# A two-layer decoder trunk: the first pair of seven-product steps of a feed-forward stage one step later, and a combination's scaling three units behind it

## The chip, the cores and the metric

One core of a Trainium2 chip runs the whole program in one launch. The metric is device microseconds of that core, as the median of several runs. Engine names are those of the profile: PE multiplies matrices (PEld is its weight load), DVE and ACT are the two elementwise engines, POOL here mostly issues transfers, SP issues the weight loads. Instructions of one engine run in the order in which the program emits them; engines wait for each other through semaphores.

## What is computed

The reference, cut to what matters here, for 256 tokens, model width 2048 and two layers:

```
for l in range(DEPTH):
    h = rms_norm(x, norm1_g[l])
    z = h @ w_in[l]
    ...
    x = x + mix @ w_out[l]
    h2 = rms_norm(x, norm2_g[l])
    x = x + jnp.square(jax.nn.relu(h2 @ w_up[l])) @ w_down[l]
return rms_norm(x, final_g)
```

`w_up` is 2048 x 8192 and `w_down` 8192 x 2048. The change touches the last line of the loop alone, the feed-forward part.

## The kernel before

**Weights and their split.** Each float32 weight tile is split into a high part (ACT, `hi`, L167 or L185) and the rest (DVE, `lo`, L177 or L190), and each product is three matmuls: high by high, low by high, high by low. The unit of planning is one weight tile of 128 x 1024 numbers. SP loads it into one of 7 `raw` buffers; there are 6 `hi` and 6 `lo` buffers. The main loop (L993 to L1014) emits, ahead of the matmuls of a step, the `hi` of tiles up to five ahead and the `lo` of tiles up to four ahead.

**Plain steps.** `transposed` (L369) makes channel-major steps: one weight tile as the stationary operand, 24 matmuls (L400, L402, L404), results with channels on the partitions. Here they are called plain steps.

**Seven-product steps.** `fast` (L407) does a 512-column part of `w_down` for one stage with Strassen-like sums: seven products in place of eight, with tokens on the partitions. Each such part is a pair of steps, p = 0 and p = 1. A step has four tiles: top, bottom, and two sums of weights (upper, lower) that DVE makes from the raw tiles in place (L218, L219 ahead of the upper `hi`, L222, L223 behind it). It issues 36 matmuls (L430, L432, L433); the six of its seventh product are held back (`left_over`) and come in the plain step behind it, after that step's first three.

**The stages.** The hidden width is cut into 8 stages of 1024. Stage e computes its part of `w_up` (16 plain steps, four per 256 columns) and uses the hidden values of stage e - 1 for `w_down`: some plain steps, and three pairs (groups 0, 1 and 2, for output columns 0 to 511, 512 to 1023 and 1024 to 1535). Before which plain steps of a stage the two steps of each pair stand is a table (L63 to L66): `USUAL` for stages 2 to 6, `ORDER` for stages 1, 7 and 8. In a usual stage group 1 stands before plain steps 1 and 2, group 2 before 6 and 7, group 0 before 11 and 14. In stage 7 group 1 stands before 1 and 2, group 0 before 6 and 9, and there is no group 2. Plain steps 0 to 3 make up the first 256 columns of `w_up`; behind step 3 their result is taken out of PSUM (L780, or L782 in stage 7), squared (L783) and split (L640 on ACT, L643 on DVE).

**Sums of the activations.** The products of a pair also need sums of hidden values; `sums` (L793) makes them on DVE (L796 to L799), and `parts` splits them (L640 and L643 on the tile `shared`). They are emitted near the end of a stage and are first used by group 1 of the next.

**Results of the pairs.** Groups 1 and 2 accumulate over stages in DRAM (`far`): behind the second step of a pair `other_done` (L879) copies three PSUM banks to `stage` (L897, three ACT instructions), two steps later the seventh product (L883), and POOL adds them to `far` (L862), or in the last stage of a group adds `far` to `stage` (L893). Group 0 stays in PSUM.

**The combination.** When a group is complete (group 2 in stage 6, groups 1 and 0 in stage 7), `combine` (L808) adds the seven products on DVE (L814 to L822), scales the four results by the squared norm factor on ACT (L825), and some units later `turn_back` transposes them on PE (L835) and adds them to `x` (L499). `soon(n, fn)` emits `fn` at the first step that starts at least n units later; a plain step is one unit, a seven-product step four.

Of the kernel before, what the change touches and what calls it, by code (L numbers as in the profile page):

```python
# [31 lines left out]
AF = mybir.ActivationFunctionType  # L32
# [27 lines left out]

ORDER = {1: ((7, 10), (13, 14)), 7: ((6, 9), (1, 2)), 8: ()}  # L63
FINAL = (7, 7, 6)
LAST = (4, 6, 8, 10, 0, 2, 12, 14)
USUAL = ((11, 14), (1, 2), (6, 7))  # L66
WARM = 11
HALVES = 5
D_SCORES, D_NORM, D_TURN, D_VALUES = 2, 1, 3, 2
# [21 lines left out]
def trunk(ctx: ExitStack, tc: tile.TileContext, layout, xT, consts, gains, w, b_sp, w_sp, out):  # L91
# [11 lines left out]
    vec, act, pe = nc.vector, nc.scalar, nc.tensor  # L103
# [142 lines left out]
    def soon(delay, fn):  # L246

        due.append((now[0] + delay, fn))
# [258 lines left out]
    def layer(l, n1, n2, n3, last):  # L507
# [218 lines left out]
        d = 0  # L726
        if l == 0:
            d = 9
# [79 lines left out]
        def combine(place, c, banks, o=None):  # L808

            d1, d2, d3, d5, d7, d6, d4 = (place[:, 256 * n:256 * (n + 1)] for n in range(7))  # L810
            p1, p2, p3, p5, p7, p6, p4 = o or (d1, d2, d3, d5, d7, d6, d4)
            if o:
                act.activation(d1, p1, AF.Copy)
            vec.tensor_tensor(d2, d1, p2, op=OP.add)  # L814
            vec.tensor_tensor(d6, d1, p6, op=OP.add)
            vec.tensor_tensor(d7, d6, p7, op=OP.add)
            vec.tensor_tensor(d6, d6, p5, op=OP.add)
            vec.tensor_tensor(d3, d6, p3, op=OP.add)
            vec.tensor_tensor(d4, d7, d4, op=OP.subtract)
            if o:  # L820
                vec.tensor_tensor(d4, d4, p4, op=OP.subtract)
            vec.tensor_tensor(d7, d7, p5, op=OP.add)  # L822
            for tt, out in enumerate(((d2, d3), (d4, d7))):
                for d in out:
                    act.activation(d, d, AF.Copy, scale=n2.r2[:, tt:tt + 1])  # L825
            wait = 6 if o else 7
            soon(wait, lambda: turn_back(c, d2, d4, banks[0]))
            soon(wait + (1 if o else 2), lambda: turn_back(c + 2, d3, d7, banks[1]))

        def turn_back(c, first, second, bank):  # L830
            ps = bank()
            for j in range(2):
                for tt, src in enumerate((first, second)):
                    o = j * S + tt * P
                    pe.transpose(ps[:, o:o + P], src[:, j * P:(j + 1) * P], ident)  # L835
            soon(1, lambda: update(n3, c, ps, False, last))
# [31 lines left out]
        def first_done(e):  # L868
            def f(o):
                if e < 7:  # L870
                    soon(5, lambda: seventh_out(e, o))
                else:
                    soon(10, lambda: nc.gpsimd.dma_start(stage[:, 1536:1792], far[0]))
                    soon(14, lambda: combine(stage, 0, [aux_bank] * 2, o))
                    for i, c in enumerate((12, 14)):
                        soon(17 + 2 * i, lambda c=c: rest_in(c))
            return f

        def other_done(e, g, banks):  # L879
            here = [lambda i=i: acc_bank(i) for i in (2, 3)]  # L880

            def rest(o):
                act.activation(stage[:, 1536:1792], o[6], AF.Copy)  # L883
                for i in range(4):
                    soon(2 * i, lambda r=slice(512 * i, min(512 * (i + 1), 1792)): move(r))
                if e == FINAL[g]:
                    soon(9, lambda: combine(stage, 4 * g, here))

            def move(r):
                if e < FINAL[g]:  # L890
                    put(e, g, r)
                else:
                    nc.gpsimd.dma_start(stage[:, r], far[g][:, r], accum_op=OP.add)  # L893

            def f(o):
                for i in (2, 0, 1):
                    act.activation(stage[:, 512 * i:512 * (i + 1)], banks[i], AF.Copy)  # L897
                soon(5, lambda: rest(o))
            return f

        base = len(steps)
        for e in range(9):
# [3 lines left out]
            if e:  # L906
                w = 512 * len(ORDER.get(e, USUAL))
                hidden = [hid[e - 1]]
# [3 lines left out]
                               cols=None if e < 8 else [c * P for c in LAST])  # L912
                for g, at in enumerate(ORDER.get(e, USUAL)):
                    banks = []
# [147 lines left out]
```

## Time and profile before

| | us |
|---|---|
| three runs | 2038.5, 2039.89, 2045.22 (median 2039.89) |
| the profiled execution: its own time | 2044.94 |
| its span (first to last instruction) | 2042.6 |
| PE busy in the span | 2027.5 (99%) |
| DVE busy | 1579.3 (77%) |
| ACT busy | 1214.8 (59%) |
| POOL busy | 156.8 (8%) |

The span is 2.3 us shorter than the execution's own time; the profiled execution was 5.05 us above the median of the runs. A row of the timeline gives the start in the span, the duration, engine, line, operation, output and inputs, shapes, and the idle time ahead of it with what ended it. Equal instructions without a gap are merged (x2): the duration is then from the first one's start to the last one's end, and neighbours overlap a little.

### The profile page before, as it was taken

What the parts mean: (1) busy time and instruction counts of PE and PEld (TensorE: products, weight loads), DVE (VectorE), ACT (ScalarE), POOL (GpSimd) and SP (SyncE); (2) the same over time, 40 slices, a digit from 0 to 9 for tenths busy, and PEclk for the clock granted to TensorE, in tenths of its full rate; (3) what the DMA queues carried; (4) which work ended last, traced back from release to release, by engine and by line L of the source; (5) the groups of instructions that cost most, each with busy time, mean ns of one, the idle gap of its engine ahead of it and who ended that gap; (6) DMA issues with size and microseconds to landing.
All of it is one profiled execution on the core that took longest, in us unless ns stands there. A gap on an engine that the chain in (4) does not pass through costs nothing.

```text
span 2042.6 us, 40747 instructions
## 1 busy us (share of the span) xinstructions
PE 2027.5 (99%) x16834; PEld 1988.6 (97%) x16834; DVE 1579.3 (77%) x1950; ACT 1214.8 (59%) x1613; POOL 156.8 (8%) x200
## 2 busy tenths in 40 slices
PE   9999999999999999999999999999999999999997
PEld 8998999999999999999989989999999999999997
DVE  7566765788888888888855667667888888888985
ACT  7565455666675665765545554556665766667654
POOL 0002300001010010100000023000010100100000
PEclk9999999999999999999999999999999999999999
DMA  9555556567586776865565555555676866868562
GB/s 326 191 166 167 184 193 203 168 233 220 196 260 206 227 220 193 241 214 202 197 216 172 169 176 191 191 191 178 217 231 199 272 190 216 256 197 259 184 217 84
DMA packets 126442, 419.26 MB, mean 205 GB/s; under 512 B 14128, under 2 KB 22064, under 8 KB 126256
## 3 DMA queue, kind: packets, MB, share of 16 engines
q1 hardware_dynamic: 110800, 389.86, 56.3%
q0 software_dynamic: 14304, 23.86, 6.4%
q8 instruction: 131, 2.15, 0.4%
q10 hardware_dynamic: 1152, 2.94, 0.4%
q14 instruction: 55, 0.45, 0.1%
HBM read 394.58 MB, written 22.02 MB: 204 GB/s over the span
## 4 chain that ended last, share of the span: by engine, by line
PE 91%; DVE 5%; ACT 2%; issue 1%; DMA 1%; ACTq 0%; DVEq 0%; SPq 0%
PE acc L402 22%; PE acc L404 22%; PE acc L400 22%; PE acc L461 3%; PE acc L459 3%; PE acc L460 3%; PE aux L430 3%; PE aux L433 3%; PE aux L432 3%; PE acc L430 2%; PE acc L432 2%; PE acc L433 2%; DVE lo L177 2%; ACT hi L167 1%; DVE shared L643 1%
## 5 line engine op out<-in xcount | busy, mean ns | idle before, releaser
L167 ACT ACTIVATE hi<-raw 128x1024 fp32r<-128x1024 f32 (+1 forms) x817 | 836.8, 1050 | 516.2 <-DVE raw L219 233.9
L177 DVE TENSOR_TENSOR lo<-raw,hi 128x1024 fp32r<-128x1024 f32 (+1 forms) x817 | 965.0, 1213 | 155.8 <-ACT hi L167 153.6
L400 PE MATMUL acc<-hs,hi 128*128 128x256 f32 x2816 | 784.4, 279 | 0.0
L402 PE MATMUL acc<-hs,lo 128*128 128x256 f32 x2816 | 782.5, 278 | 0.4
L404 PE MATMUL acc<-hs,hi 128*128 128x256 f32 x2816 | 781.3, 277 | 0.0
L402 PEld LDWEIGHTS acc<-hs,lo 128*128 128x128 f32 x2816 | 529.2, 188 | 2.7 <-DVE lo L177 2.0
L400 PEld LDWEIGHTS acc<-hs,hi 128*128 128x128 f32 x2816 | 530.8, 189 | 0.4 <-issue 0.2
L404 PEld LDWEIGHTS acc<-hs,hi 128*128 128x128 f32 x2816 | 529.0, 188 | 0.0
L400 PE MATMUL acc<-half,hi 128*128 128x256 f32 x1344 | 373.0, 278 | 2.3 <-ACT hi L167 2.3
L402 PE MATMUL acc<-half,lo 128*128 128x256 f32 x1344 | 372.0, 277 | 0.0
L404 PE MATMUL acc<-half,hi 128*128 128x256 f32 x1344 | 372.0, 277 | 0.0
L400 PEld LDWEIGHTS acc<-half,hi 128*128 128x128 f32 x1344 | 252.8, 188 | 2.6 <-ACT hi L167 2.6
L402 PEld LDWEIGHTS acc<-half,lo 128*128 128x128 f32 x1344 | 252.6, 188 | 0.0
L404 PEld LDWEIGHTS acc<-half,hi 128*128 128x128 f32 x1344 | 252.4, 188 | 0.0
L862 POOL DMA_DIRECT2D far<-ar x92 | 74.7, 983 | 1168.2 <-ACT ar L865 620.7
L432 PE MATMUL acc<-lo,shared 128*128 128x256 f32 x384 | 107.4, 280 | 0.0
L433 PE MATMUL acc<-hi,shared 128*128 128x256 f32 x384 | 106.6, 277 | 0.0
L430 PE MATMUL acc<-hi,shared 128*128 128x256 f32 x384 | 106.5, 277 | 0.0
L643 DVE TENSOR_TENSOR half<-ar,half 128x512 fp32r<-128x512 f32 x72 | 49.7, 691 | 67.8 <-ACT half L640 67.6
L459 PE MATMUL acc<-hi,hs 128*128 128x512 f32 x256 | 101.7, 397 | 0.0
L461 PE MATMUL acc<-hi,hs 128*128 128x512 f32 x256 | 100.7, 393 | 0.0
L460 PE MATMUL acc<-lo,hs 128*128 128x512 f32 x256 | 100.0, 390 | 0.5 <-DVE lo L177 0.5
(163 smaller groups left out, 2563.3 us busy)
## 6 DMA issues: line engine op xcount, KB each, us to landing
raw<-in_w SPq DMA_DIRECT2D x731, 512.0 KB, 4.6
far<-ar POOLq DMA_DIRECT2D x60, 256.0 KB, 7.4
far<-ar POOLq DMA_DIRECT2D x32, 128.0 KB, 5.1
ar<-far POOLq DMA_DIRECT2D x12, 256.0 KB, 8.6
raw<-in_w SPq DMA_DIRECT2D x10, 256.0 KB, 4.8
x<-in_xT SPq DMA_DIRECT2D x7, 256.0 KB, 6.0
out<-x SPq DMA_DIRECT2D x7, 256.0 KB, 3.1
shared<-in_b_sp ACTq DMA_DIRECT2D x2, 512.0 KB, 7.7
```

Source lines behind the costliest of these rows:

```text
L167: act.activation(self.h[:, j * m:(j + 1) * m], self.raw[:, j * m:(j + 1) * m], AF.Copy)
L177: vec.tensor_tensor(lo[:, r], self.raw[:, r], self.h[:, r].bitcast(F32), op=OP.subtract)
L400: pe.matmul(o, lhsT=hi, rhs=xs[:, 0, :], start=(k0 + k == 0 and (two or cb == 0)), stop=False, skip_group_check=True)
L402: pe.matmul(o, lhsT=wt.lo[:, k, cb * P:(cb + 1) * P], rhs=xs[:, 0, :], start=False, stop=False, skip_group_check=True)
L404: pe.matmul(o, lhsT=hi, rhs=xs[:, 1, :], start=False, stop=last, skip_group_check=True)
L430: pe.matmul(o[n], lhsT=xh, rhs=hi, start=(p == 0 and k == 0 and n in fresh), stop=False, skip_group_check=True)
L432: pe.matmul(o[n], lhsT=xh, rhs=lo, start=False, stop=False, skip_group_check=True)
L433: pe.matmul(o[n], lhsT=xl, rhs=hi, start=False, stop=(n in last and p == 1 and k == 1), skip_group_check=True)
L459: pe.matmul(ps, lhsT=xh, rhs=hi, start=(k0 + k == 0), stop=False)
L460: pe.matmul(ps, lhsT=xh, rhs=lo, start=False, stop=False)
L461: pe.matmul(ps, lhsT=xl, rhs=hi, start=False, stop=(k0 + k == KC - 1))
L862: nc.gpsimd.dma_start(far[g][:, r], src, **({} if e == max(g, 1) else {"accum_op": OP.add}))
```

## The change

Two edits. The table puts the two steps of group 1 one plain step later, in the usual stages and in stage 7. And `combine` no longer emits its four scalings at once, but through `soon(3, ...)`.

```
-ORDER = {1: ((7, 10), (13, 14)), 7: ((6, 9), (1, 2)), 8: ()}
+ORDER = {1: ((7, 10), (13, 14)), 7: ((6, 9), (2, 3)), 8: ()}
-USUAL = ((11, 14), (1, 2), (6, 7))
+USUAL = ((11, 14), (2, 3), (6, 7))
...
-            for tt, out in enumerate(((d2, d3), (d4, d7))):
-                for d in out:
-                    act.activation(d, d, AF.Copy, scale=n2.r2[:, tt:tt + 1])
+
+            def scale():
+                for tt, out in enumerate(((d2, d3), (d4, d7))):
+                    for d in out:
+                        act.activation(d, d, AF.Copy, scale=n2.r2[:, tt:tt + 1])
+
+            soon(3, scale)
             wait = 6 if o else 7
```

Behind this place the lines of the changed kernel have numbers larger by 4 (L883 becomes L887, L897 becomes L901); the scaling L825 becomes L827. No instruction is added or dropped.

In the rows below `acc` and `aux` are PSUM banks, `ar` is the scratch tile that `stage` is a part of, `half` the split hidden values, `shared` their split sums, and `nr` the squared norm factor; numbers behind a name tell buffers apart.

ACT in stage 3 of layer 0, before: from the copies behind group 1's second step to the `hi` tiles of group 2's first step. The two tiles behind the copies are those of plain steps 4 and 5; L185 is the top tile of group 2, the two behind it bottom and upper, the last two lower and the tile of plain step 6.

```order
L897 ACTIVATE ar<-acc_6390 128x512
L897 ACTIVATE ar<-acc_6388 128x512
L897 ACTIVATE ar<-acc_6389 128x512
L167 ACTIVATE hi<-raw 128x1024 x2
L185 ACTIVATE hi<-raw 128x512
L167 ACTIVATE hi<-raw 128x1024 x2
L883 ACTIVATE ar<-aux 128x256
L780 ACTIVATE ar<-acc_6357 128x512
L783 ACTIVATE ar<-ar 128x512
L640 ACTIVATE half<-ar 128x2x256
L167 ACTIVATE hi<-raw 128x1024 x2
```

The same place on ACT in the changed kernel, where the single tile behind the copies is that of plain step 5.

```order
L901 ACTIVATE ar<-acc_6420 128x512
L901 ACTIVATE ar<-acc_6418 128x512
L901 ACTIVATE ar<-acc_6419 128x512
L167 ACTIVATE hi<-raw 128x1024
L185 ACTIVATE hi<-raw 128x512
L167 ACTIVATE hi<-raw 128x1024 x2
L780 ACTIVATE ar<-acc_6357 128x512
L783 ACTIVATE ar<-ar 128x512
L640 ACTIVATE half<-ar 128x2x256
L167 ACTIVATE hi<-raw 128x1024
L887 ACTIVATE ar<-aux 128x256
L167 ACTIVATE hi<-raw 128x1024
```

Between the copies and group 2's top tile one plain tile is gone (it stands ahead of the copies now), and the seventh product's copy moved from ahead of L780 to behind the lower tile; the rest is as it was.

ACT in stage 7 of layer 0, before, where group 0 is combined: L813 copies the first product, L825 are the four scalings.

```order
L640 ACTIVATE shared<-ar 128x2x256 x2
L167 ACTIVATE hi<-raw 128x1024
L813 ACTIVATE ar<-aux 128x256
L825 ACTIVATE ar<-ar,nr_3823 128x256 x4
L167 ACTIVATE hi<-raw 128x1024 x6
```

The same place on ACT in the changed kernel.

```order
L640 ACTIVATE shared<-ar 128x2x256 x2
L167 ACTIVATE hi<-raw 128x1024
L813 ACTIVATE ar<-aux 128x256
L167 ACTIVATE hi<-raw 128x1024 x3
L827 ACTIVATE ar<-ar,nr_3823 128x256 x4
L167 ACTIVATE hi<-raw 128x1024 x3
```

Three of the six tiles behind the scalings now stand ahead of them.

## The prediction

> **What bounds the kernel now.** I began with the page's busy times and the waits of PE, then went to stretches of time, one per feed-forward stage, and last to the timelines of ACT and DVE at the two places that the change moves.
>
> ```profile
> PE 2027.5 (99%) x16834; PEld 1988.6 (97%) x16834; DVE 1579.3 (77%) x1950; ACT 1214.8 (59%) x1613; POOL 156.8 (8%) x200
> ```
>
> Whom PE's weight loads wait for: us in total, times, longest.
>
> ```profile
> PEld acc L400 <- ACT hi L167: 2.6, 2, 1.3
> PEld acc L402 <- DVE lo L177: 2.0, 8, 0.3
> PEld aux L321 <- DVE nr L347: 1.3, 1, 1.3
> ```
>
> PE is the bound almost everywhere, and none of these waits is for a transfer. Nothing of its work is removed, so the change can act only through moments in which PE waits: two of 1.3 us that end with ACT's `hi` (L400), and eight of up to 0.3 us that end with DVE's `lo` (L402). The windows below are whole stages: stage 5 of layer 0, stage 5 of layer 1, then stages 2 and 3 of layer 0. Each has the same 732 matmuls; the count in a window takes in those that overlap its edges.
>
> ```profile
> 715.53:801.62 86.09, 86.09 (x735) 86.09 (x733) 73.05 (x83) 54.45 (x70) 7.89 (x9) 1.00 0.72 219
> 1728.24:1812.12 83.88, 83.83 (x735) 83.55 (x734) 72.80 (x83) 54.50 (x70) 7.77 (x9) 1.00 0.72 225
> 462.19:545.51 83.32, 83.32 (x734) 83.32 (x733) 68.58 (x77) 52.42 (x67) 6.65 (x9) 1.00 0.71 226
> 545.51:629.35 83.84, 83.79 (x734) 83.52 (x733) 72.78 (x83) 54.48 (x70) 7.88 (x9) 1.00 0.73 225
> ```
>
> Stage 2 is undisturbed: 83.32 us, 0.1135 us for a matmul. Stage 3 and stage 5 of layer 1 take 0.52 and 0.56 us more; this is what the small waits for `lo` at group 1 cost, since PE also runs a little slower just behind a wait. Stage 5 of layer 0 has no idle time at all and yet takes 86.09 us, 0.1171 us for a matmul, at the same granted clock of 1.00. So there are slow stretches of about 3% inside "busy" time.
>
> [...]
>
> **The change part by part: group 1 one step later.** Gain first. In eight of the twelve stages that are moved PE waits for `lo` at group 1 (the eight waits above). One more plain step ahead gives PE 24 x 0.1135 = 2.72 us more to do and DVE one `lo` more, which starts 1.13 us before the next (below). Group 1 gets about 1.6 us of slack, more than the 0.5 that it lacks. Gain: 8 x 0.55 = 4.4 us.
>
> Now what comes behind. This is ACT in stage 3 of layer 0, from the end of group 1 to group 2's first step. The last matmul of group 1's second step releases the first copy at 560.25; PE goes on with the plain step at 560.07, and times below count from there.
>
> ```profile
> 560.27 1.58 ACT L897 ACTIVATE ar<-acc 128x512 f32<-128x512 f32 x3 [0.43 <-PE acc L433]
> 561.72 2.02 ACT L167 ACTIVATE hi<-raw 128x1024 fp32r<-128x1024 f32 x2
> 563.62 0.64 ACT L185 ACTIVATE hi<-raw 128x512 fp32r<-128x512 f32 x1
> 564.14 1.07 ACT L167 ACTIVATE hi<-raw 128x1024 fp32r<-128x1024 f32 x1
> 568.36 1.06 ACT L167 ACTIVATE hi<-raw 128x1024 fp32r<-128x1024 f32 x1 [3.15 <-DVE raw L219]
> 569.33 0.36 ACT L883 ACTIVATE ar<-aux 128x256 f32<-128x256 f32 x1
> 569.59 0.59 ACT L780 ACTIVATE ar<-acc 128x512 f32<-128x512 f32 x1
> ...
> 571.42 2.00 ACT L167 ACTIVATE hi<-raw 128x1024 fp32r<-128x1024 f32 x2
> ```
>
> And DVE there, as far as group 2's second step:
>
> ```profile
> 559.13 2.35 DVE L177 TENSOR_TENSOR lo<-raw,hi 128x1024 fp32r<-128x1024 f32 x2
> 562.83 2.36 DVE L177 TENSOR_TENSOR lo<-raw,hi 128x1024 fp32r<-128x1024 f32 x2 [1.35 <-ACT hi L167]
> 565.11 0.68 DVE L190 TENSOR_TENSOR lo<-raw,hi 128x512 fp32r<-128x512 f32 x1
> 565.71 1.22 DVE L177 TENSOR_TENSOR lo<-raw,hi 128x1024 fp32r<-128x1024 f32 x1
> 566.84 0.68 DVE L218 TENSOR_TENSOR raw<-raw 128x512 f32<-128x512 f32 x1
> 567.56 0.69 DVE L219 TENSOR_TENSOR raw<-raw 128x512 f32<-128x512 f32 x1
> ...
> 572.50 2.36 DVE L177 TENSOR_TENSOR lo<-raw,hi 128x1024 fp32r<-128x1024 f32 x2 [0.26 <-ACT hi L167]
> ...
> 579.29 4.77 DVE L177 TENSOR_TENSOR lo<-raw,hi 128x1024 fp32r<-128x1024 f32 x4
> ```
>
> This is one chain, and the end of group 1 starts it. ACT may copy the banks only when group 1's second step is done; the next `hi` tiles queue behind the copies; DVE stands idle for 1.35 us for the first of them, then runs to L219; ACT stands idle for 3.15 us for L219, with L883, L780 and the lower tile queued behind the waiting upper tile; and so on to the `lo` of plain step 6 (ready at 572.50 + 2.36 = 574.86, 14.79 after the start) and of plain step 7 (the third of the four at 579.29: 584.06 less one start distance of 1.13 is 582.93, 22.86 after the start).
>
> PE needs them after a number of matmuls: behind group 1 come one plain step with the seventh product (30), n more plain steps (24 each), group 2's first step (36) and one matmul. With n = 3 that is 139, or 15.78 us: the `lo` of step 6 is 0.99 us early. For step 7 (66 more) it is 23.27 us: 0.41 early. So group 2 has hardly any slack now.
>
> The change makes n = 2. PE arrives 2.72 us earlier on the same clock: at 13.05 and 20.54. The chain loses one `lo` only, 1.13 us: by the order, its other instructions are the same, and the copy of the seventh product merely changes its place. The `hi` of step 6 ended at 571.42 + 2.00, 13.35 after the start; now at 12.22; its `lo` follows in 0.03 + 1.22: 13.47, or 0.42 late. The way from there to step 7's `lo` is 582.93 - 574.86 = 8.07: 21.54, or 1.00 late in all. Per usual stage that is 1.0 us of PE, ten times: 10.0. It also meets stage 2, where group 1 lost nothing. In stage 7 group 0's second step comes only at 9, so the lateness ends with step 6: between 0.42 and 1.0, I take 0.7, twice: 1.4. After the last late `lo` PE runs slower for some us, as behind the waits at group 1: 0.1 us per stage, 1.1. Together 12.5; from outside, 0.5 us a stage (half of the chain's lateness, if copies and tiles pack closer than now) gives 6, and 1.3 gives 15.
>
> The stages of a slow stretch lose less: at 0.1171 step 7's `lo` is needed at 181 x 0.1171 = 21.20, 0.34 late. In this execution these were stages 4 to 6 of layer 0 (the rows of 4 and 6 follow; 5 is above), some 2 us less in all.
>
> ```profile
> 629.35:715.53 86.18, 86.13 (x735) 85.86 (x734) 73.39 (x83) 54.90 (x70) 7.89 (x9) 1.00 0.71 219
> 801.62:888.39 86.77, 86.77 (x742) 86.77 (x741) 75.95 (x92) 55.91 (x74) 7.96 (x9) 1.00 0.70 217
> ```
>
> POOL's four transfers of group 1 start from the same copies, 2.72 us later; the copies wait for PE in the row above, not for a transfer that still reads `stage`, so I count the transfers at nothing, and the weight loads too, which SP issues in an order that shifts by one tile. In stage 7 group 1's combination moves a step as well, to group 0's second step; ahead of the `lo` of step 9 it stands as before, so nothing; without that cover its seven additions cost 7 x 0.42 = 2.9 us per layer at most (duration below).
>
> **The scaling.** It goes with the two waits of 1.3 us, one per layer. Here is the one in layer 0, first on ACT.
>
> ```profile
> 966.31 0.51 ACT L825 ACTIVATE ar<-ar,nr 128x256 f32<-128x256 f32 x1 [2.54 <-DVE ar L814]
> 968.00 0.51 ACT L825 ACTIVATE ar<-ar,nr 128x256 f32<-128x256 f32 x1 [1.19 <-DVE ar L818]
> ...
> 970.56 1.04 ACT L167 ACTIVATE hi<-raw 128x1024 fp32r<-128x1024 f32 x1
> ```
>
> Then DVE, with one of the combination's additions, and PE.
>
> ```profile
> 967.55 0.42 DVE L818 TENSOR_TENSOR ar<-ar,aux 128x256 f32<-128x256 f32 x1
> ...
> 970.14 0.69 DVE L761 TENSOR_TENSOR acc<-acc,nR 128x512 f32<-128x512 f32 x1
> 970.87 0.69 DVE L499 TENSOR_TENSOR x<-x,acc 128x512 f32<-128x512 f32 x1
> ```
>
> ```profile
> 971.70 0.36 PE L400 MATMUL acc<-half,hi 128*128 128x256 f32 x1 [1.15 <-ACT hi L167]
> ```
>
> ACT waits 2.54 + 1.19 us inside the scalings, the `hi` tiles come late, and PE's wait is put down to the `hi` that ends at 971.60. But this matmul opens a new column, and its PSUM bank is read by L499, which ends at 971.56: 0.04 us earlier. L499 stands behind the combination's additions on DVE, and those don't move. So what is late next is the bank: gain 0.04 of 1.3 us, nothing. If I am wrong about the bank it is 2 x 1.2 = 2.4. The scalings now come three units (8 us) later and four of 0.5 us end well before the transposes, which stay six or seven units behind the combination; a cost would have to exceed the 8 us left.
>
> **The sum.** The profiled execution: 2044.94 - 4.4 + 12.5 - 2.0 = 2051.0. It is 5.05 us above the median of the runs. I take this difference for a longer slow stretch (three stages at 86.09 - 83.32 = 2.77 us are 8.3) and carry it over: 2039.89 + 6.1 = 2046.0. With no slow stretch the 2.0 would come back and the gain grow by two stages, 1.1; half of this difference, since the median run has about half of the stretch, is 0.4: 2046.4.
>
> **The rivals.** A measurement of this kernel can tell about 0.3% from no change, 6.1 us: 2033.8 to 2046.0.
>
> *It cancels.* The lateness at group 2 is real but nearer to 0.7 us, or PE spends more stages in the slow pace, where it hardly waits: 12 stages of 0.7 less 4.4 is +4, 2043.9. For it: the slack that is lacking is a difference of 13 us long chains. Also here belongs no effect at all. [...] The eight waits for `lo` speak against it.
>
> *Faster.* One mechanism: a wait at group 1 can leave PE in the slow pace for several stages (stage 5 of layer 0 has no wait of its own). If the change takes away what starts these stretches and the new waits start none, the time falls by 4.4 and by the stretches of the median run (8.3 - 5.05, and stage 7's part, some 4 us in all): 2031.5. It decides if the lateness at group 2 stays below 0.2 us a stage. The chain above speaks against that.
>
> *Worse.* Three late `lo` tiles per stage in place of two put PE into the slow pace more often: 2.77 us for each further stage; three more give 2054.7.
>
> **The numbers.** Forecast, slower by over 0.3%, from 2046.0 up: 0.40, and the worse case 0.07. It cancels: 0.43. Faster: 0.10. The forecast's own range is 2046 to 2052; the range for eight in ten goes down into the cancelling case and up to the worse one, 2037.0 to 2053.5.
>
> **What would show it.** Right: the waits of PE for `lo` move from group 1 to plain step 6, group 2's second step and step 7, in all usual stages, stage 2 among them; stage 2 takes about 84.4 in place of 83.32 us; the 1.3 us waits ahead of stage 8 stay and are put down to DVE's L499. Wrong: stage 2 unchanged, or the long waits gone.

## The result, and the profile after

| | before | after |
|---|---|---|
| median of seven runs each, us | 2039.34 | 2047.64 |
| lowest, highest | 2037.29, 2045.22 | 2046.15, 2050.87 |
| the profiled execution: its own time, span | 2044.94, 2042.6 | 2047.64, 2045.2 |

The ratio is 1.004, with an interval of 1.0027 to 1.0053: the changed kernel is slower by some 8 us. A run of either kernel can hold stretches in which PE is about 3% slower, as the prediction describes them: 86.09 in place of 83.32 us for the 732 matmuls of a stage, or 0.1176 and 0.1138 us for one. Two single runs apart (2950.24 us for before, 8724.36 for another kernel below), the times of one kernel lie up to 21 us apart, and in the profiled runs these stretches make up most of the difference, so the lowest times and the stages without a stretch are compared beside the medians.

The page says next to nothing: PE is 99% busy as before, and DVE and ACT are as busy as they were.

```profile
PE 2024.2 (99%) x16834; PEld 1982.0 (97%) x16834; DVE 1580.5 (77%) x1950; ACT 1217.6 (60%) x1613; POOL 157.2 (8%) x200
```

The waits of PE's weight loads tell more. There were 8 waits for `lo`, 2.0 us in all and 0.3 at most; now there are 24, up to 1.5 us. The two for `hi` are as they were.

```profile
PEld acc L402 <- DVE lo L177: 10.8, 24, 1.5
...
PEld acc L400 <- ACT hi L167: 2.6, 2, 1.3
```

The 24 stand where the prediction put them, two in each of the ten usual stages (0.46 us at plain step 6, 0.23 at step 7; a third at group 2's second step stays below 0.1), and two in each stage 7, at step 6 and, against the prediction, at step 9. Those of stage 3 of layer 0, then of stage 7 of layer 1:

```profile
PEld acc L402 <- DVE lo L177: 0.7, 2, 0.5
```

```profile
PEld acc L402 <- DVE lo L177: 2.0, 2, 1.5
```

Whole stages again: 2, 3 and 5 of layer 0, then 5 and 7 of layer 1. All usual stages take the same time now, and no stretch of the slow pace lasts for a stage.

```profile
462.57:546.93 84.36, 84.08 (x734) 83.58 (x733) 69.54 (x78) 54.32 (x70) 6.64 (x9) 1.00 0.71 224
546.93:631.30 84.37, 84.09 (x734) 83.59 (x733) 72.86 (x83) 54.71 (x69) 7.87 (x9) 1.00 0.74 224
715.67:800.03 84.36, 84.08 (x734) 83.58 (x733) 72.95 (x83) 54.70 (x69) 7.89 (x9) 1.00 0.72 224
1727.76:1812.12 84.36, 84.07 (x734) 83.67 (x733) 72.86 (x83) 54.68 (x69) 7.77 (x9) 1.00 0.73 223
1897.40:1986.79 89.39, 86.56 (x755) 85.79 (x754) 77.77 (x99) 52.34 (x66) 4.08 (x5) 1.00 0.63 200
```

Stage 2 went from 83.32 to 84.37 (84.36 in its row, by the rounding of its ends), 1.05 more; stage 5 of layer 1 from 83.88 to 84.36, 0.5 more, since there the gain of group 1 is taken off. Stage 7 of layer 1 was this in the kernel before; it lost 1.50:

```profile
1896.86:1984.75 87.89, 86.70 (x754) 85.91 (x753) 77.67 (x99) 53.39 (x69) 4.07 (x5) 1.00 0.64 209
```

Without slow stretches the sum is 10 x 1.05 for the usual stages, less 8 x 0.53 for group 1 (stages 3 to 6), plus 2 x 1.5 for stage 7: 10.5 - 4.2 + 3.0 = 9.3 us. The lowest runs are 2046.15 - 2037.29 = 8.9 apart, and the span of the changed kernel, 2045.2, is 9.4 longer than the 2035.8 of the run with the scaling alone (below), which has before's order and no stretch.

Here is the chain behind group 1 in stage 3 of layer 0 of the changed kernel. ACT first, from the three copies (L897 before, L901 now) to the `hi` of step 6:

```profile
564.20 1.58 ACT L901 ACTIVATE ar<-acc 128x512 f32<-128x512 f32 x3 [2.14 <-PE acc L433]
...
571.16 1.07 ACT L167 ACTIVATE hi<-raw 128x1024 fp32r<-128x1024 f32 x1 [2.97 <-DVE raw L219]
...
575.15 1.05 ACT L167 ACTIVATE hi<-raw 128x1024 fp32r<-128x1024 f32 x1
```

Then DVE: its idle time behind the copies, the `lo` of step 6 (the second of two), the `lo` of step 7 (the third of four).

```profile
566.75 1.22 DVE L177 TENSOR_TENSOR lo<-raw,hi 128x1024 fp32r<-128x1024 f32 x1 [3.06 <-ACT hi L167]
...
575.01 2.44 DVE L177 TENSOR_TENSOR lo<-raw,hi 128x1024 fp32r<-128x1024 f32 x2 [0.26 <-ACT hi L167]
...
581.89 4.77 DVE L177 TENSOR_TENSOR lo<-raw,hi 128x1024 fp32r<-128x1024 f32 x4
```

The first copy starts 0.20 us behind the end of group 1, as before (560.27 and 560.07), so the chain counts from 564.00. The `lo` of step 6 is ready at 577.45, 13.45 after that, that of step 7 at 586.66 - 1.13 = 585.53, 21.53 after. The prediction gave 13.47 and 21.54. PE waits:

```profile
577.51 0.39 PE L402 MATMUL acc<-hs,lo 128*128 128x256 f32 x1 [0.26 <-DVE lo L177]
```

### The profile page after: what moved, and what is told of

Same layout as the page of the kernel before. It is cut to its first block, busy times and chain, and to the rows that moved or that the text cites. A ratio compares the mean times of both kernels' runs of the same rounds, so it can differ in the third digit from the quotient of the medians.

```text
span 2045.2 us, 40727 instructions
## 1 busy us (share of the span) xinstructions
PE 2024.2 (99%) x16834; PEld 1982.0 (97%) x16834; DVE 1580.5 (77%) x1950; ACT 1217.6 (60%) x1613; POOL 157.2 (8%) x200
## 4 chain that ended last, share of the span: by engine, by line
PE 89%; DVE 4%; ACT 4%; issue 2%; DMA 0%; SPq 0%; ACTq 0%; DVEq 0%
PE acc L402 22%; PE acc L404 21%; PE acc L400 21%; PE acc L461 3%; PE acc L459 3%; PE acc L460 3%; PE acc L432 3%; PE acc L433 3%; PE acc L430 3%; ACT hi L167 2%; PE aux L430 2%; PE aux L433 2%; PE aux L432 2%; DVE lo L177 2%; ACT ar L901 1%
## 5 line engine op out<-in xcount | busy, mean ns | idle before, releaser
L402 PE MATMUL acc<-hs,lo 128*128 128x256 f32 x2816 | 780.8, 277 | 5.9 <-DVE lo L177 5.7
L400 PE MATMUL acc<-hs,hi 128*128 128x256 f32 x2816 | 781.3, 277 | 0.0
L402 PEld LDWEIGHTS acc<-hs,lo 128*128 128x128 f32 x2816 | 528.8, 188 | 11.2 <-DVE lo L177 10.8
L400 PEld LDWEIGHTS acc<-hs,hi 128*128 128x128 f32 x2816 | 528.8, 188 | 0.3 <-issue 0.2
L400 PE MATMUL acc<-half,hi 128*128 128x256 f32 x1344 | 372.0, 277 | 2.3 <-ACT hi L167 2.3
L402 PE MATMUL acc<-half,lo 128*128 128x256 f32 x1344 | 371.0, 276 | 0.0
L400 PEld LDWEIGHTS acc<-half,hi 128*128 128x128 f32 x1344 | 252.3, 188 | 2.6 <-ACT hi L167 2.6
L402 PEld LDWEIGHTS acc<-half,lo 128*128 128x128 f32 x1344 | 252.3, 188 | 0.0
L432 PE MATMUL acc<-lo,shared 128*128 128x256 f32 x384 | 106.8, 278 | 0.0
L643 DVE TENSOR_TENSOR half<-ar,half 128x512 fp32r<-128x512 f32 x72 | 49.8, 691 | 65.6 <-ACT half L640 65.4
```

What stands on the lines that cost most here:

```text
L400: pe.matmul(o, lhsT=hi, rhs=xs[:, 0, :], start=(k0 + k == 0 and (two or cb == 0)), stop=False, skip_group_check=True)
L402: pe.matmul(o, lhsT=wt.lo[:, k, cb * P:(cb + 1) * P], rhs=xs[:, 0, :], start=False, stop=False, skip_group_check=True)
L432: pe.matmul(o[n], lhsT=xh, rhs=lo, start=False, stop=False, skip_group_check=True)
```

## The experiments

All times are medians of twelve runs unless said otherwise (five of the last kernel). Each group ran beside the kernel before on its own chip, and before's median there was 2039.02 (first group), 2044.97 (second), 2047.79 (third) and 2037.54 us (last). These differ by more than most edits, most likely through slow stretches; so an edit is judged by the stages that it touches, and the whole by the ratio to before on the same chip.

| kernel | median | lowest | ratio to before (interval) |
|---|---|---|---|
| order alone | 2049.29 | 2046.06 | 1.004 (1.0025 to 1.0055) |
| scaling alone | 2040.62 | 2037.23 | 1.0005 (0.9988 to 1.0023) |
| stage 7 as before | 2045.5 | 2043.54 | 1.0023 (1.0008 to 1.0038) |
| two copies held back | 2042.03 | 2034.4 | 1.0002 (0.998 to 1.0024) |
| group 1's combination behind a `lo` | 2049.69 | 2045.98 | 1.0026 (1.001 to 1.0043) |
| group 0's combination later | 2046.56 | 2042.94 | 1.0013 (0.9993 to 1.0034) |
| groups 1 and 2 later | 2045.98 | 2045.53 | 1.0007 (0.9988 to 1.0027) |
| the same, stage 7 as before, group 0's combination later | 2041.36 | 2040.05 | 0.9993 (0.9969 to 1.0016) |
| three edits together | 2041.19 | 2028.55 | 0.9951 (0.9929 to 0.9973) |
| and a column's relu, square, rounding later | 2041.9 | 2033.69 | 0.9987 (0.9961 to 1.0013) |
| before, with group 0's combination later | 2042.8 | 2034.66 | 0.9988 (0.997 to 1.0005) |
| three edits and the square, rounding later | 2029.34 | 2028.0 | 0.996 (0.9947 to 0.9974) |

**The two halves of the change.** First the order alone:

```
-            soon(3, scale)
+            scale()
```

> The changed kernel with the scaling back at its old place, straight behind a combination's additions: the change of the order alone. My theory (the whole loss is the chain of copies, hi and lo tiles into group 2, plus group 1's combination ahead of step 9 in stage 7): the same as the changed kernel, 2047.6, within 1.5 us, and stage 2 of layer 0 at 84.37. Rival A (moving the scaling costs something): nearer to before, 2044 or less. Rival B (the scaling gains, and hides a larger loss of the order): above 2050.

It came out at 2049.29, stage 2 at 84.37: the changed kernel. The profiled run, 2049.26, holds a stretch of the slow pace (stage 3 of layer 0, 85.95); that stretches explain the slightly higher median as well isn't shown. Then the scaling alone, on the table of before:

> The kernel before with only the scaling emitted three units behind the combination. My theory: the same as before, 2039.4, within 1 us; the two waits of 1.3 us ahead of stage 8 stay although ACT's hi tiles come earlier. Rival A (the scaling costs): 2042 or more. Rival B (the hi tiles were what PE waited for): 2.4 us less, 2037.0, and the two waits gone.

2040.62 and a ratio of 1.0005: nothing that can be told from zero. PE's two waits ahead of stage 8 stay, and the trace, free of long stretches, shows all waits at group 1. There are twelve, but not one for each of the twelve stages: stage 2 has none, stages 3 to 6 have one each and stage 7 has two.

```profile
PEld acc L402 <- DVE lo L177: 3.1, 12, 0.3
PEld acc L400 <- ACT hi L167: 2.6, 2, 1.3
```

So the whole loss is the table's.

**Stage 7 back at its old step.**

```
-ORDER = {1: ((7, 10), (13, 14)), 7: ((6, 9), (2, 3)), 8: ()}
+ORDER = {1: ((7, 10), (13, 14)), 7: ((6, 9), (1, 2)), 8: ()}
```

> The changed kernel with stage 7's group 1 back at its old step; the ten usual stages stay changed. The trace of the changed kernel shows stage 7 of layer 1 1.49 us longer than before, and 1.5 us of that at step 9, where DVE's lo stands behind the additions of group 1's combination. My theory: 1.49 x 2 = 3.0 us less than the changed kernel, 2044.6 (2043.6 to 2045.6), with stages 2 to 6 still at 84.37 (85.28 the sixth). Rival (stage 7 loses nothing of its own, the usual stages carry all): 2047.6.

2045.5, between the theory's 2044.6 and the rival's 2047.6 but within its range of 2043.6 to 2045.6; the lowest run is 2.6 below that of the changed kernel. Stage 7 of layer 1:

```profile
1895.82:1983.89 88.07, 86.88 (x755) 86.09 (x753) 77.83 (x99) 53.44 (x69) 4.08 (x5) 1.00 0.64 209
```

1.3 us less than the changed kernel's 89.39. Stage 7 does lose for itself: 1.3 by this run, 1.5 by the kernel before.

**Two of the three copies held back**, into ACT's idle time ahead of the upper tile's `hi`:

```
-                for i in (2, 0, 1):
-                    act.activation(stage[:, 512 * i:512 * (i + 1)], banks[i], AF.Copy)
+                copy(2)
+                pending.extend([lambda i=i: copy(i) for i in (0, 1)])
...
                 vec.tensor_tensor(t.right(), b.right(), t.right(), op=OP.subtract)
+                run_pending()
             Sub.high(self, 1)
```

> The changed kernel with two of a group's three copies (the banks that don't hold its last product) held back on ACT until just ahead of the next upper tile's hi, that is, into the 3 us in which ACT stands idle for L219; only the third copy is still ahead of the hi tiles behind group 1. My theory (the chain that begins with three copies decides): it becomes about 2 x 0.5 = 1.0 us shorter up to DVE's lo of steps 6 and 7, so the 1.05 us per stage go nearly whole: stage 2 at 83.3 to 83.5, stage 7 about 0.5 less, in all 10 to 11.8 us less than the changed kernel, 2036 to 2037.6. Rival A (what is late is DVE's own queue, or the transfers behind group 1, and not ACT's copies): no change, 2047.6. Rival B (PE's slow stretches are the loss, and have nothing to do with the chain): stage 2 stays at 84.37.

The mechanism held and the median did not. PE's waits for `lo` fell from 24 to 2, both in stage 7 (L402 is L408 here):

```profile
PEld acc L408 <- DVE lo L177: 2.9, 2, 1.5
```

Stages without a slow stretch take 83.39, so 0.98 of the 1.05 is gone, and nothing but ACT's copies had moved. Others in the same execution take 86.10, stage 5 of layer 1 for one:

```profile
462.37:545.76 83.39, 83.39 (x735) 83.38 (x733) 69.63 (x78) 54.33 (x70) 6.67 (x9) 1.00 0.72 226
...
1724.70:1810.80 86.10, 86.10 (x735) 86.10 (x733) 73.12 (x83) 54.75 (x69) 7.81 (x9) 1.00 0.73 219
```

The lowest run, 2034.4, is 11.75 below the changed kernel's lowest, as forecast; the median, 2042.03, is not, for the stretches. Rival A falls.

**Group 1's combination in stage 7 behind the `lo` of step 9.**

```
-                    soon(9, lambda: combine(stage, 4 * g, here))
+                    soon(10 if e == 7 else 9, lambda: combine(stage, 4 * g, here, early=2 * (e == 7)))
...
-            wait = 6 if o else 7
+            wait = (6 if o else 7) - early
```

> The changed kernel; in stage 7 alone group 1's combination is emitted one unit later, so that its seven additions stand behind DVE's lo of step 9 and not ahead of it; its transposes keep their place. My theory (the additions delay that lo): the wait of 1.5 us at step 9 goes, in both layers, stage 7 of layer 1 at about 87.9, 3.0 us less than the changed kernel, 2044.6 (2043.6 to 2045.6); the rest of stage 7's loss, 0.9 us ahead of step 9, stays. Rival (that lo is late by the chain that begins with the three copies, and the additions only stand beside it): 2047.6 and the wait stays.

The stage did as expected, the run did not: stage 7 of layer 1 takes 87.94 in place of 89.39, the wait of 1.5 us is gone, and the longest wait for `lo` that is left is 0.5.

```profile
1902.71:1990.65 87.94, 86.28 (x754) 85.71 (x753) 77.89 (x99) 52.30 (x66) 4.08 (x5) 1.00 0.62 204
```

The median of 2049.69 is 5 us above the forecast, and the lowest run, 2045.98, is no lower than the changed kernel's 2046.15. The profiled run holds slow stretches in five usual stages and in stage 7 of layer 0 (stage 3 of layer 0 85.94, of the changed kernel 84.37). Stage by stage they make this run 6.9 us longer: without them its 2050.58 would be 2043.6, the lower end of the forecast's range. For the other eleven runs, which have no trace, the same is argued, not shown. The two waits ahead of stage 8 grew to 1.5 us each.

**Group 0's combination one unit later**, so that DVE does L761 and L499 ahead of its additions:

```
-                    soon(14, lambda: combine(stage, 0, [aux_bank] * 2, o))
+                    soon(15, lambda: combine(stage, 0, [aux_bank] * 2, o))
```

> The changed kernel; group 0's combination is emitted one unit later, so that L761 and L499, which free the bank of the matmul that waits ahead of stage 8, stand ahead of the combination's additions on DVE. ACT's hi tiles keep their place ahead of the scalings. Bank theory: both waits of 1.3 us ahead of stage 8 go, 2.5 us less than the changed kernel, 2045.1 (2044.4 to 2046.0). Rival (PE waits for ACT's hi, as the profile puts it): the waits stay, 2047.6.

Both waits of 1.3 us ahead of stage 8 are gone; stage 7 of layer 0 went from 89.38 to 87.99 us.

```profile
885.33:973.32 87.99, 86.30 (x755) 85.69 (x753) 76.38 (x98) 52.18 (x66) 4.14 (x5) 1.00 0.62 198
```

In the changed kernel two things end just ahead of the matmul that waits: L499 at 969.03, and a `hi` tile at 969.12, to which the profile puts the wait. DVE, ACT and PE there:

```profile
968.34 0.69 DVE L499 TENSOR_TENSOR x<-x,acc 128x512 f32<-128x512 f32 x1
```

```profile
968.06 1.06 ACT L167 ACTIVATE hi<-raw 128x1024 fp32r<-128x1024 f32 x1 [1.66 <-PE acc L404]
```

```profile
969.17 0.36 PE L400 MATMUL acc<-half,hi 128*128 128x256 f32 x1 [1.15 <-ACT hi L167]
```

With the edit L499 stands eight additions earlier. ACT's tile has not moved, and the same matmul starts at 967.88, before that tile begins:

```profile
965.21 0.69 DVE L499 TENSOR_TENSOR x<-x,acc 128x512 f32<-128x512 f32 x1
```

```profile
968.08 1.07 ACT L167 ACTIVATE hi<-raw 128x1024 fp32r<-128x1024 f32 x1 [1.66 <-PE acc L404]
```

```profile
967.88 0.28 PE L400 MATMUL acc<-half,hi 128*128 128x256 f32 x1
```

So the wait was for the PSUM bank, and the `hi` named by the profile belongs to a later step. The median, 2046.56, fell by 1.1 where 2.5 was forecast; the lowest run, 2042.94, by 3.2. In the median, then, the gain is not clear of the scatter; it is the stage that shows it.

**Group 2 one step later too**, which gives back the plain step between the groups:

```
-USUAL = ((11, 14), (2, 3), (6, 7))
+USUAL = ((11, 14), (2, 3), (7, 8))
```

> The changed kernel with group 2 moved one step later too (steps 7 and 8 in place of 6 and 7), so that again three plain steps stand between the groups; stage 7, which has no group 2, stays as changed. My theory (the loss of the usual stages is that PE reaches group 2 a plain step earlier than the chain behind group 1 allows): no wait for lo in stages 2 to 6, stage 2 at 83.32, the others as well but for 0.4 in stage 6: 10.5 us less than the changed kernel, 2037.1 (2035.6 to 2040). Rival A (group 1's later place itself costs, or group 0 becomes late in turn): above 2043. Rival B on the slow stretches: if nothing but a short wait starts one, the times of the twelve runs lie within 3 us; if they come by chance, they spread over some 15 us, as they do where two copies are held back.

My theory missed by 9 us; the time is rival A's, but by a mechanism that neither had named. The waits for `lo` in the usual stages are gone, as the theory has it; but a new wait stands in each of them:

```profile
PEld acc L400 <- ACT ar L901: 8.8, 10, 0.9
```

Step 8 opens a new column of `w_up`, so it needs a PSUM bank at once, and it is the third of those out of which group 2's products are only now copied. PE waits for the copy (here in stage 4 of layer 1):

```profile
1683.40 0.38 PE L400 MATMUL acc<-hs,hi 128*128 128x256 f32 x1 [0.69 <-ACT ar L901]
```

Stage 2 takes 84.27, hardly less than 84.37. The twelve times lie within 2.1 us. Then the same with stage 7 as before and group 0's combination later:

> Groups 1 and 2 both one step later in the usual stages, stage 7's group 1 at its old step, and group 0's combination one unit later. By my theory the sum of what the others show apart: 10.5 for the usual stages, 3.0 for stage 7, 2.5 for the waits ahead of stage 8, 16 us less than the changed kernel, 2031.6 (2030 to 2035), 8 below before. If the waits ahead of stage 8 are ACT's: 2034.1. If slow stretches come by chance: 2036 or more in the median, with a lowest run near 2031.

2041.36, 10 us above the forecast: of the 16 us the 10.5 of the usual stages fall away but for 10 x (84.37 - 84.27) = 1.0; with the 5.5 that are left it is 2041.1. The parts add up. Two of the twelve times, 2060.66 and 8724.36, lie far above the others, which end at 2043.04; the median of those ten is 2040.8.

**Three edits together** (copies held back, group 1's combination in stage 7 behind the `lo`, group 0's combination later):

> The changed kernel with three edits together: two of the three copies held back, stage 7's combination of group 1 behind the lo of step 9, group 0's combination one unit later. By the runs of each apart the lowest time is 2034.4 (copies) less 3.0 (step 9) less 2.5 (the waits ahead of stage 8): 2028.9, and these parts do not overlap. If slow stretches are started by PE's last short waits (0.07 us at step 7, where the lo is just in time), the median lies as far above the lowest as with the copies alone, 7.6 us: 2036.5, and the runs spread over some 15 us. Rival (stretches come from stage 7's long waits): median within 3 us of the lowest.

The lowest run, 2028.55, is as forecast; the median, 2041.19, is 4.7 above the 2036.5 of the forecast. The times lie in two bunches, five from 2028.55 to 2029.96 and seven from 2041.17 to 2043.57. The profiled run (2041.38) shows what is between them: layer 0 has no slow stretch, layer 1 has one from stage 2 to the end of stage 6. Stage 4 of each:

```profile
629.27:712.67 83.40, 83.40 (x734) 83.38 (x733) 72.95 (x83) 54.71 (x69) 7.93 (x9) 1.00 0.75 226
1636.86:1722.95 86.09, 86.09 (x734) 86.09 (x733) 73.13 (x83) 54.76 (x69) 7.82 (x9) 1.00 0.74 219
```

Five such stages of one layer are 12.1 us over in this run (the first is slow in part). The rival is out: stage 7's long waits are gone (85.48 us in both layers) and the stretch is there.

**Relu, square and rounding of the first column later**, on top of the three edits, so that the `lo` of step 7 no longer is just in time:

```
+            if 1 < e < 7:
+                return lambda c, ps: soon(1, lambda: f(c, ps)) if c == 0 else f(c, ps)
             return f
```

> The same three edits, and in stages 2 to 6 the first column's relu, square and rounding on ACT (L780 and behind it) are emitted one unit later, behind the next hi tile and not ahead of it: the lo of steps 6 and 7 no longer wait for them, and come some 0.5 us or more ahead of need in place of 0.07 behind it. My theory (the queue order on ACT decides, and a short wait starts a slow stretch): no wait for lo in stages 2 to 6, stage 2 at 83.3, lowest time 2028.2, and the runs within 5 us, median 2031 or less. If stretches come by chance, without a wait: lowest 2028.2, median near 2036, spread some 15 us. Rival (the late relu keeps a PSUM bank from group 2): a new wait on a copy, 1 us per stage, lowest 2038.

A miss. The three instructions moved behind one `hi` and now stand straight ahead of the next, which is that of step 6; DVE in turn waits 0.86 us for the rounding, ahead of the same tile's `lo`:

```profile
1671.87 0.69 DVE L649 TENSOR_TENSOR half<-ar,half 128x512 fp32r<-128x512 f32 x1 [0.86 <-ACT half L646]
1672.82 1.22 DVE L177 TENSOR_TENSOR lo<-raw,hi 128x1024 fp32r<-128x1024 f32 x1 [0.26 <-ACT hi L167]
```

Stages of layer 1 take 83.9, and the waits for `lo` are back (eight, up to 0.3). It shows the queue order at work, against me. The times spread over 21 us, and in the profiled run layer 0 is in the slow pace from stage 3 to the end of stage 6.

**Before with group 0's combination later alone:**

> The kernel before with one edit: group 0's combination one unit later, so that L761 and L499 stand ahead of its additions on DVE. Bank theory: the two waits ahead of stage 8 go as they did on the changed kernel, 2.5 us less than before, ratio 0.9988, waits for lo at group 1 as before. Rival (there ACT's hi is late as well, since the scalings stand ahead of it in the kernel before; but a combination that comes later moves them too): 0 to 1 us.

The ratio is 0.9988, as forecast, with an interval (0.997 to 1.0005) that takes in 1. So the time alone doesn't show the gain. The trace does: it has eight small waits for `lo` and none for L400, and stage 7 of layer 1, 87.89 in the kernel before, takes 86.31.

```profile
1896.24:1982.55 86.31, 86.26 (x755) 85.81 (x753) 76.12 (x97) 53.20 (x69) 4.09 (x5) 1.00 0.64 209
```

**Three edits, and only the square and the rounding later**, behind group 2's tiles; the relu, which frees the bank, keeps its place:

```
                 def rest(h=hid[e][0]):
                     act.activation(z, z, AF.Square)
                     to_half(h, c // P, z, True)

                 if 1 < e < 7 and c == 0:
                     soon(4, rest)
                 else:
                     rest()
```

> The three edits together, and in stages 2 to 6 the square and the rounding of the first column (not its relu, which frees the PSUM bank) are emitted four units later on ACT, behind group 2's hi tiles; nothing of ACT's 1.25 us and of the low part on DVE stands then ahead of the lo of steps 6 and 7. My theory (the queue order decides): the lo of step 7 some 1 us ahead of need, where it was 0.07 behind; no wait for lo in stages 2 to 6, stage 2 at 83.32, lowest time 0.7 below that of the three edits (2028.55): 2027.9. If a short wait is what starts a slow stretch, all twelve runs lie within 3 us, median 2028 to 2030, about 10 below before's lowest. If stretches come without a wait: in some runs a whole layer is slow, 12.7 us each, median 2040 as with the three edits. Rival (the later square delays another tile): a wait for lo behind group 2.

All as the theory has it: median 2029.34, five runs from 2028.0 to 2029.88, ratio 0.996 (0.9947 to 0.9974), so 8 us faster than before, and the ratio of the change itself was 1.004. Stages 2 to 5 take 83.32, as the undisturbed stage did (stage 5 of layer 1, with one matmul more, 83.43). In stage 3 of layer 0 the `lo` of step 7 ends at 581.94, 1.4 us before its matmul at 583.33; with the three edits alone these were 583.50 and 583.57. Stage 4 of the two layers:

```profile
628.95:712.27 83.32, 83.32 (x734) 83.32 (x733) 72.93 (x83) 54.60 (x69) 7.91 (x9) 1.00 0.75 226
1631.91:1715.23 83.32, 83.32 (x734) 83.32 (x733) 72.92 (x83) 54.58 (x69) 7.82 (x9) 1.00 0.75 226
```

The longest wait of PE's weight loads is no longer in a feed-forward stage at all:

```profile
PEld aux L327 <- DVE nr L353: 1.3, 1, 1.3
```

Before itself lay within 1.0 us on this chip (2037.02 to 2038.03 in nine runs), though its kept trace has short waits, so the narrow spread does not prove that short waits start the slow stretches. Against the three edits, on another chip, only the lowest times can be set side by side: 2028.0 and 2028.55, 0.55 apart where 0.7 was forecast.

## Why the prediction was right, and where it was not

- *The chain behind group 1, 1.0 us a stage and 0.1 of tail.* Right: 1.05 measured, with both `lo` tiles ready within 0.02 us of the forecast. The experiment with two copies held back takes 0.98 of it away, so the loss comes through the copies that stand ahead of the `hi` tiles on ACT. One input was read wrongly without effect: the prediction divided a stage's time by its row's count, 734 or 735, which takes in matmuls at the edges. By the 732 of a stage a matmul takes 0.1138 us, in the slow pace 0.1176, and the times at which PE needs the `lo` move by less than 0.1 us.
- *Group 1's gain, 0.55 a stage.* Right: 0.53, as stage 3 with its wait (83.85 in the run with the scaling alone) and stage 2 without one (83.32) show. The eight waits are not one a stage: stage 7 of layer 1 has two of them, and stage 6 of layer 1 waits at group 1 in another line (L432, 0.2 us). That they are as many as the eight stages that wait is luck.
- *The scaling, nothing.* Right, within the scatter, and shown apart by the run with the scaling alone. The reason holds too: it is the bank behind L499. But that the profile would then name L499 was wrong; PE's row still says `hi`. (More on that at the end.)
- *Stage 7.* Here a step failed: that the lateness ends with step 6, 0.7 us, and that "ahead of the `lo` of step 9 it stands as before, so nothing" of group 1's combination. DVE before, in stage 7 of layer 1, from the first and the last of its seven additions:

```profile
1935.06 0.42 DVE L814 TENSOR_TENSOR ar<-ar 128x256 f32<-128x256 f32 x1
...
1937.56 0.43 DVE L822 TENSOR_TENSOR ar<-ar 128x256 f32<-128x256 f32 x1
1937.90 1.22 DVE L177 TENSOR_TENSOR lo<-raw,hi 128x1024 fp32r<-128x1024 f32 x1
1939.04 0.69 DVE L643 TENSOR_TENSOR half<-ar,half 128x512 fp32r<-128x512 f32 x1
1939.64 4.62 DVE L177 TENSOR_TENSOR lo<-raw,hi 128x1024 fp32r<-128x1024 f32 x4
```

The same after, and PE's wait at step 9:

```profile
1936.77 1.21 DVE L177 TENSOR_TENSOR lo<-raw,hi 128x1024 fp32r<-128x1024 f32 x1
1938.21 0.69 DVE L643 TENSOR_TENSOR half<-ar,half 128x512 fp32r<-128x512 f32 x1 [0.23 <-ACT half L640]
1938.82 0.42 DVE L814 TENSOR_TENSOR ar<-ar 128x256 f32<-128x256 f32 x1
...
1941.33 0.42 DVE L822 TENSOR_TENSOR ar<-ar 128x256 f32<-128x256 f32 x1
1941.67 8.03 DVE L177 TENSOR_TENSOR lo<-raw,hi 128x1024 fp32r<-128x1024 f32 x7
```

```profile
1942.94 0.39 PE L402 MATMUL acc<-hs,lo 128*128 128x256 f32 x1 [1.32 <-DVE lo L177]
```

The additions stand ahead of the `lo` of step 9 in both kernels, as the prediction has it; one `lo` that stood behind them now stands ahead. But the lateness does not end with step 6, since DVE has hardly any idle time up to there in which to catch up (0.23 us, ahead of L643 in the rows above): counted from the stage's start, the `lo` of step 9 begins at 1939.64 - 1896.86 = 42.78 before and at 1941.67 - 1897.40 = 44.27 after, 1.49 later, which is what the stage lost. PE's own times from the stage's start, ahead of the last matmuls of group 0's first step, just behind step 6's wait and just behind step 9's, are 30.18, 31.10 and 44.27 before and 29.36, 31.20 and 45.76 after: 0.82 gained at group 1, 0.92 lost at step 6, 1.40 lost at step 9. The prediction had a gain of 0.55, a loss of 0.7 + 0.1 at step 6 and nothing at step 9, 0.25 in all; so 1.25 too little per layer, 2.5 for both. That the additions are what can be moved out of the way is shown by the experiment that puts them behind this `lo`. With the copies held back alone the wait stays, 1.5 us: there PE comes earlier by about as much as the `lo` does.
- *The slow stretches.* The 2051.0 for the profiled execution, made with stretches that stay, was 3.4 too high: this execution of the changed kernel has none that lasts, 84.37 where stage 4 took 86.18. The median, 2047.64, lies 1.2 above the forecast of 2046.4, less than the 2.5 that stage 7 was short. That is luck: before's median over seven runs came out 0.55 lower than over the three that the forecast began from, and the usual stages lost 1.05 and not 1.1.
- *The rivals.* "It cancels" fails on the size of the lateness, 1.05 and not 0.7, and on stage 7. "No effect" fails on the order alone (1.004): with DVE 77% busy and ACT 60%, the order of their queues cost 0.4%. "Faster" asked for less than 0.2 us at group 2. "Worse", more slow stretches, did not happen in the profiled run.

## What to carry to other kernels

When a step is moved, measure the chain from what it releases to the next step that needs the same queues, and look behind that step until the late engine next has idle time: in stage 7 DVE, late at step 6, began the `lo` of step 9 still 1.49 us later than before. What stands ahead of a needed tile in an in-order queue decided more here than how busy the engine was: with four such places changed together, the changed kernel became 0.4% faster than the kernel before. And a move that clears one wait can meet the next resource: with group 2 later it was a PSUM bank (up to 0.9 us, ten times), with the relu, square and rounding one unit later the next tile in the same queue (eight waits for `lo`, up to 0.3 us). Moving the square and the rounding behind all of group 2's tiles, and leaving the relu in its place, met none.

## What the runs showed of the hardware that was not expected

- PE has a slower pace, 86.09 us for the same stage as 83.32 (0.1176 and 0.1138 us for a matmul), at a granted clock of 1.00 in both. In the kernel before a stretch of it begins at group 1's second step in stage 4 of layer 0, where matmuls start 0.16, 0.23 and 0.32 us behind the one ahead of them (641.81, 642.04 and 644.24), in place of 0.113; it is still there in stage 5, which has no wait, and in stage 6. With the three edits one runs through the five usual stages of layer 1 and costs 12.1 us. Lateness alone did not start one: gaps of 0.14, 0.23 and 0.33 us in stage 3 of the kernel before (557.96, 558.19 and 560.40), of up to 0.40 in its layer 1 (1659.26), and of 1.60 in stage 7 of the changed kernel (1942.94) have no stretch behind them. What decides that is open.
- Where the slow pace ends, the traces show two things, if the first microsecond behind a wait is left aside: a later matmul that comes late, as at a wait for `lo` (in the changed kernel the slow pace from 1505.46 on ends behind the wait at 1513.31), or four transposes of a combination (L835). In the kernel before the slow stretch of layer 0 has 0.118 us from one matmul to the next up to the transposes at 882.50 and 0.113 behind them, and the one in stage 7 changes in the same way at those at 945.46; both had passed a first four, at 876.41 and 939.37, without a change. No run moves the transposes or leaves them out, so that they end a stretch is not shown.
- The profile puts PE's two waits of 1.3 us ahead of stage 8 (1.5 with group 1's combination moved) to ACT's `hi` in all eight kernels that have them, though the bank behind DVE's L499 was what they were for; only in the one with group 1's combination moved does the matmul's own row name L499. There L499 ended 0.06 us behind the `hi` tile (971.77 and 971.71); in the kernel before and in the changed one it ended 0.04 and 0.09 us ahead of it (971.56 and 971.60, 969.03 and 969.12).
